# FFN up projection: four products of 512 columns and four of 256 per row tile, in four banks

## Chip, core and metric

The kernel runs on one core of a Trainium2 chip. The metric is the device time of one execution in microseconds (us). A core has TensorE (PE, matrix products into PSUM), VectorE (DVE), ScalarE (ACT), GpSimd (POOL) and SyncE (SP, which issues the loads here). PSUM has eight banks of 512 FP32 columns.

## What is computed

One block of a diffusion transformer on 256 latent and 256 context tokens of width 2048, in FP32. The first half (a modulated norm, an input projection, three mixers and an output projection) matters here only as what lies before. The second half is a convolutional FFN on the latent tokens:

```
def _conv_ffn(h, w_up, conv_w, conv_b, w_down, rows, width):
    gate, val = jnp.split(h @ w_up, 2, axis=-1)
    gate = lax.conv_general_dilated(gate.reshape(bsz, rows, width, D_FF), conv_w[:, :, None, :],
                                    (1, 1), 'SAME', feature_group_count=D_FF) + conv_b
    return (jax.nn.gelu(gate.reshape(bsz, l, D_FF)) * val) @ w_down

h_lat = h_lat + m_lat[5] * _conv_ffn(_modulate(h_lat, norm2_g[i], m_lat[3], m_lat[4]),
                                     ffn_w_up[i], ffn_conv_w[i], ffn_conv_b[i], ffn_w_down[i], rows, GRID_W)
return _rmsnorm(h_lat, norm_f)
```

(Calls are shortened.) `D_FF` is 5632, the grid has 4 rows of 64 tokens. `m_lat` are six vectors of 2048 made from the condition by a product with `ada_w`; `m_lat[5]` is the gate of the FFN.

## The kernel before

Activations lie with features on the 128 partitions and the 256 tokens along the free axis. FP32 products are made from a high and a low part of each operand: `split_w` (line 452) loads a block of weights (256 x 512, 512 KB), casts it to the type fp32r (ACT, line 457: the high part) and subtracts that from the block (DVE, line 459: the low part). `prod` (line 462) then makes three products into one place of PSUM: high weights by high activations (line 464), high by low (465), low by high (466). Every product loads its stationary operand (128 x 128 weights) anew and streams the activations.

`gemm_feat` (line 484) makes one group: 512 output columns over some blocks of weights, for each block two row tiles (128 input features each) by four blocks of 128 output columns. Its four sums, 256 tokens wide, share two PSUM banks (`two_banks`, line 472), taken in turn from a pool of four (`mm`). Another pool of three (`sm`) and one of a single bank (`ad`) serve the other tasks.

The FFN (`up` at line 1392, `down` at line 1422) has 11 units of 512 hidden features. `up(u)` makes a gate group and a value group of eight blocks each. The convolution reads the gate sums from PSUM: one scaled copy with bias (ACT, line 1403) and eight multiply-adds (DVE, line 1411) for each of four output blocks, in a buffer of the small pool `t`; then GELU, the product with the value sums (line 1418) and a split into high and low parts (lines 469 and 470). `down(g)` makes four groups over the hidden features of two units (of the last one alone) and adds them into `dsum` (lines 1437, 1439). The order is up 0, up 1, up 2, down 0, up 3, up 4, down 1, and so on. Activations for the up projection lie in eight tiles `f_t` (line 1352), four of high and four of low parts.

Vectors of `m_lat` are made beside that. `ada_vector` (line 419) is a task in turns: each turn loads 512 KB and multiplies and adds it on DVE (line 433), two halves of 16 turns; after each half two products with ones add up over partitions, into the bank `ad`. Two of the vectors are made so in the earlier stage, driven from its loops, and the last, the FFN gate, in the down groups (`t_gate`, line 1381). There its first half has to give back its buffer before the second can begin. Loads pass through rings of pages; the FFN uses four pages each for raw, high and low weights (line 1371) and three for `ada_w`.

A scheduler orders each engine's instructions before the run. It takes the order of the program as a priority, with the splitting of weights ahead by an offset (line 453); each engine runs its own list in order. So an edit in one task can change the neighbours on any engine.

Of the kernel before, what the change touches and what calls it, by code (L numbers as in the profile page):

```python
# [11 lines left out]
F32R = mybir.dt.float32r  # L12
AF = mybir.ActivationFunctionType
# [205 lines left out]
def tile_dit(ctx: ExitStack, tc: tile.TileContext, I, out: bass.AP, dbg=None):  # L219
# [198 lines left out]

    def ada_vector(c, after=None):

        ps = ada_bank()
        for half in range(2):
            tag = pages.take(4)
            acc = slot(tag, [P, 2, 512])
            if after is not None:

                V.tensor_copy(acc[:, 0, 0:1], after)
# [15 lines left out]
        ada_store(c, ps)  # L443
        yield

# [25 lines left out]

    def two_banks():
        bk = [mm_bank(), mm_bank()]
        return bk, lambda m: bk[m // 2][:, 256 * (m % 2):256 * (m % 2) + 256]
# [8 lines left out]

    def gemm_feat(w, cg, mv, between, kcs=None):
        kcs = list(range(8)) if kcs is None else kcs
        bk, at = two_banks()
# [864 lines left out]

    f_t = [[slot(pages.take(4), [P, 4, L], F32R) for _ in range(4)] for _ in range(2)]

    def f_of(kt):
        return f_t[0][kt // 4][:, kt % 4, :], f_t[1][kt // 4][:, kt % 4, :]

# [23 lines left out]

    t_gate = _Task(ada_vector(3, dsum[0][:, 0, 0:1]))

# [4 lines left out]
    def gated(cg):  # L1387
        for mt in range(4 * cg, 4 * cg + 4):
            V.scalar_tensor_tensor(h_of(mt), dsum[cg // 2][:, mt % 8, :], ada_cols[:, 3, mt:mt + 1], h_of(mt),
                                   ALU.mult, ALU.add)  # L1390

    def up(u, between):
        hd = hidden(u)
        bk, at = gemm_feat(I["w_up"], u, f_of, between)
        act = []
        for pr in range(2):
            acc = tb([P, 2, L])
            for e in range(2):
                m = 2 * pr + e
                mt = 4 * u + m  # L1400
                src = at(m).rearrange("p (r c) -> p r c", r=4)
                dst = acc[:, e, :].rearrange("p (r c) -> p r c", r=4)
                S.activation(acc[:, e, :], at(m), AF.Identity, bias=cw[:, 9, mt:mt + 1], scale=cw[:, 4, mt:mt + 1])  # L1403
                for dy in (-1, 0, 1):
# [98 lines left out]
```

## Time and profile before

| what | value |
|---|---|
| median of 3 runs | 1484.7 us (1481.24 to 1485.41) |
| the profiled execution | 1485.74 us, its span 1484.0 us |
| PE busy, products | 1429.8 us (96%), 11060 |
| DVE busy | 1070.7 us (72%) |
| ACT busy | 664.5 us (45%) |
| data moved | 318.57 MB, mean 215 GB/s |

Busy means that an engine had an instruction running. Products overlap in the pipeline of PE, so their durations add up to more than the time; the distance between the starts of neighbours is what one costs. The span is the profiled part of an execution, 1.7 us shorter than its time. FP32 products count twice in the profile. A granted clock of 1.00 is 2.4 GHz, 0.50 is 1.2 GHz.

### The profile page before, as it was taken

The page shows a single profiled execution, that of the slowest core. Times are in us where ns is not written, and L with a number is a line of the kernel's source. Part 1 is how long each engine was busy: PE and PEld are TensorE (multiplying, and loading weights), DVE is VectorE, ACT ScalarE, POOL GpSimd, SP SyncE. Part 2 cuts the span into 40 slices and gives each one's busy share as a digit, 9 for nine tenths or more (in the row PEclk, how much of TensorE's full clock was granted, in tenths as well). Part 3 has the DMA queues.
Part 4 walks back from the last instruction along what each step waited for, and adds up shares of the span by engine and source line. Part 5 has one row for each costly group of instructions (what it writes and reads, how often), then busy time and mean ns, then how long its engine had stood idle before and what let it go on. Part 6 is the DMA issues. An engine that isn't in the chain of part 4 may idle for free.

```text
span 1484.0 us, 27112 instructions
## 1 busy us (share of the span) xinstructions
PE 1429.8 (96%) x11060; PEld 1314.1 (89%) x11060; DVE 1070.7 (72%) x1774; ACT 664.5 (45%) x984; POOL 10.9 (1%) x9
## 2 busy tenths in 40 slices
PE   6998999999899999998999999999999999999997
PEld 3566696668888989998999999999999999999997
DVE  6568618997877888764867777675768787657766
ACT  6336851222568434343554444443444344434434
POOL 0000000000000000000000000000000000000000
PEclk9999999999999999998999999999999999999998
DMA  9788635667777787555465598666557866566552
GB/s 355 256 309 282 220 134 186 195 191 268 251 261 241 263 279 271 172 169 159 141 184 181 177 316 282 183 185 185 182 184 230 302 203 192 182 180 185 181 171 98
DMA packets 89956, 318.57 MB, mean 215 GB/s; under 512 B 12039, under 2 KB 12584, under 8 KB 89384
## 3 DMA queue, kind: packets, MB, share of 16 engines
q1 hardware_dynamic: 89832, 316.85, 65.1%
q8 instruction: 86, 1.41, 0.4%
q14 instruction: 38, 0.31, 0.1%
HBM read 312.62 MB, written 4.19 MB: 213 GB/s over the span
## 4 chain that ended last, share of the span: by engine, by line
PE 82%; DMA 7%; DVE 5%; ACT 3%; issue 2%; SPq 0%; DVEq 0%; ACTq 0%
PE mm L464 24%; PE mm L465 24%; PE mm L466 24%; DMA s4k<-in_ada_dram 6%; PE ad L410 2%; PE ad L373 2%; DVE s4k L433 1%; PE sm L579 1%; DVE s4k L459 1%; PE sm L855 1%; PE mm L339 1%; PE sm L311 1%; PE sm L549 1%; ACT s4k L457 1%; DMA s4k<-in_x_t_dram 1%
## 5 line engine op out<-in xcount | busy, mean ns | idle before, releaser
L457 ACT CAST s4k<-s4k 128x1024 fp32r<-128x1024 f32 x376 | 393.8, 1048 | 601.6 <-PE mm L465 420.7
L459 DVE TENSOR_TENSOR s4k<-s4k,s4k 128x1024 fp32r<-128x1024 f32 x376 | 459.0, 1222 | 252.8 <-ACT s4k L457 247.9
L464 PE MATMUL mm<-s4k,s4k 128*128 128x256 f32 (+1 forms) x2144 | 627.3, 295 | 4.8 <-ACT s4k L457 3.5
L466 PE MATMUL mm<-s4k,s4k 128*128 128x256 f32 (+1 forms) x2144 | 626.1, 294 | 4.9 <-DVE s4k L459 4.9
L465 PE MATMUL mm<-s4k,s4k 128*128 128x256 f32 (+1 forms) x2144 | 628.8, 294 | 1.5 <-DVE s4k L778 1.2
L464 PEld LDWEIGHTS mm<-s4k,s4k 128*128 128x128 f32 x2144 | 412.2, 193 | 28.9 <-issue 14.8
L466 PEld LDWEIGHTS mm<-s4k,s4k 128*128 128x128 f32 x2144 | 412.9, 193 | 19.9 <-DVE s4k L459 7.4
L465 PEld LDWEIGHTS mm<-s4k,s4k 128*128 128x128 f32 x2144 | 414.7, 193 | 16.4 <-issue 6.4
L464 PE MATMUL mm<-s8k,s4k 128*128 128x256 f32 x960 | 271.0, 283 | 0.8 <-ACT s8k L469 0.8
L465 PE MATMUL mm<-s8k,s4k 128*128 128x256 f32 x960 | 271.4, 283 | 0.0
L466 PE MATMUL mm<-s8k,s4k 128*128 128x256 f32 x960 | 269.9, 283 | 0.0
L464 PEld LDWEIGHTS mm<-s8k,s4k 128*128 128x128 f32 x960 | 183.9, 192 | 3.6 <-issue 2.5
L465 PEld LDWEIGHTS mm<-s8k,s4k 128*128 128x128 f32 x960 | 184.2, 192 | 0.3 <-DVE s8k L470 0.2
L466 PEld LDWEIGHTS mm<-s8k,s4k 128*128 128x128 f32 x960 | 183.5, 192 | 0.1
L433 DVE SCALAR_TENSOR_TENSOR s4k<-s4k,cs,s4k 128x1024 f32<-128x1024 f32 x90 | 115.4, 1282 | 49.2 <-DMA s4k<-in_ada_dram 48.8
L1411 DVE SCALAR_TENSOR_TENSOR t<-mm,s4k,t 128x189 f32<-128x189 f32 (+2 forms) x352 | 131.9, 423 | 7.9 <-ACT t L1403 6.3
L373 PE MATMUL ad<-s4k,cs 128*32 128x256 f32 x512 | 35.8, 393 | 6.6 <-DMA s4k<-in_ada_dram 5.8
L469 ACT CAST s8k<-t 128x512 fp32r<-128x512 f32 x38 | 23.2, 617 | 27.0 <-DVE t L1418 9.3
L373 PEld LDWEIGHTS ad<-s4k,cs 128*32 128x32 f32 x512 | 13.8, 110 | 21.2 <-DMA s4k<-in_ada_dram 7.3
L1403 ACT ACTIVATE t<-mm,s4k 128x256 f32<-128x256 f32 x44 | 24.7, 562 | 14.6 <-PE mm L466 13.6
L410 PE MATMUL ad<-s4k,cs 128*32 128x512 f32 x128 | 28.9, 604 | 1.0 <-DMA s4k<-in_ada_dram 0.5
L470 DVE TENSOR_TENSOR s8k<-t,s8k 128x512 fp32r<-128x512 f32 x38 | 25.8, 686 | 1.0
(285 smaller groups left out, 1045.2 us busy)
## 6 DMA issues: line engine op xcount, KB each, us to landing
s4k<-in_ada_dram SPq DMA_DIRECT2D x192, 512.0 KB, 4.9
s4k<-in_w_up_dram SPq DMA_DIRECT2D x176, 512.0 KB, 4.3
s4k<-in_w_down_dram SPq DMA_DIRECT2D x88, 512.0 KB, 3.7
s4k<-in_w_in_dram SPq DMA_DIRECT2D x80, 512.0 KB, 5.0
s4k<-in_w_out_dram SPq DMA_DIRECT2D x32, 512.0 KB, 3.9
s4k<-in_x_t_dram SPq DMA_DIRECT2D x8, 512.0 KB, 6.8
s4k<-in_ctx_t_dram SPq DMA_DIRECT2D x4, 512.0 KB, 10.2
hyk<-s8k SPq DMA_DIRECT2D x4, 512.0 KB, 4.1
```

The lines of the kernel that those rows point to most:

```text
L373: T.matmul(ps[32 * q:32 * q + 32, :], cs[:, 2 * k2 + e, :], raw[:, e, 256 * part:256 * part + 256], start=(k2 == 0), stop=(k2 == 7), skip_ ...
L410: T.matmul(ps[32 * q:32 * q + 32, :], cs[:, kt, :], raw[q // 2][:, q % 2, :], start=(kt == 0), stop=(kt == KT - 1), skip_group_check=True)
L433: V.scalar_tensor_tensor(acc, raw, cs[:, kt, 0:1], acc, ALU.mult, ALU.add)
L457: S.copy(h, raw)
L459: V.tensor_tensor(lo, raw, h.bitcast(F32), ALU.subtract)
L464: T.matmul(ps, a[0], b[0], start=first, stop=False, skip_group_check=True)
L465: T.matmul(ps, a[0], b[1], start=False, stop=False, skip_group_check=True)
L466: T.matmul(ps, a[1], b[0], start=False, stop=last, skip_group_check=True)
L469: S.copy(h, src)
L470: V.tensor_tensor(lo, src, h.bitcast(F32), ALU.subtract)
L1403: S.activation(acc[:, e, :], at(m), AF.Identity, bias=cw[:, 9, mt:mt + 1], scale=cw[:, 4, mt:mt + 1])
L1411: V.scalar_tensor_tensor(dst[:, r0:r1, c0:c1], src[:, r0 + dy:r1 + dy, c0 + dx:c1 + dx], cw[:, tap, mt:mt + 1], dst[:, r0:r1, c0:c1], ALU. ...
```

## The change

In the up projection the high and low activations of a row tile now lie side by side (`f_t` in eight tiles of two row tiles each), so that one product of 512 columns takes the high weights by both. `gemm_wide` makes, for each row tile, four such products (one per block of 128 output columns, each into a bank of its own, line 1429 of the new file) and then four of 256 columns with the low weights (line 1432). A group takes four banks: groups alternate between the four of `mm` and the three of `sm` with `ad` (`four_banks`). At its end ACT copies the high-by-low half out of each bank (line 1438) and DVE adds the other half (line 1439). The convolution and the product with the value now read those sums from SBUF; its result lies in a buffer `16k0`. `down` keeps `prod` and takes two banks a group from the set that the last up group left alone.

`ada_vector` loses three empty turns. The FFN gate has its own task `ada_gate2`, with one buffer for both halves and all its products with ones at the end, so that it no longer holds the bank `ad`.

```diff
-    def ada_vector(c, after=None):
+    def ada_vector(c):
...
-            yield
-            yield
             for e in range(2):
...
+            if half == 0:
+                yield
         ada_store(c, ps)
         yield
+
+    def ada_gate2(after):
+
+        acc = slot(pages.take(8), [P, 2, 2, 512])
+        V.tensor_copy(acc[:, 0, 0, 0:1], after)
+        for half in range(2):
+            for kt in range(KT):
+                raw = load_a(I["ada25"][3, kt, half])
...
+                    V.scalar_tensor_tensor(acc[:, half], raw, cs[:, kt, 0:1], acc[:, half], ALU.mult, ALU.add)
+                yield
+        yield
+        yield
+        ps = ada_bank()
+        for q in range(4):
+            T.matmul(ps[32 * q:32 * q + 32, :], ones[:, 0:1].to_broadcast([P, 32]), acc[:, q // 2, q % 2, :],
+                     start=True, stop=True, skip_group_check=True)
+        ada_store(3, ps)
...
-    f_t = [[slot(pages.take(4), [P, 4, L], F32R) for _ in range(4)] for _ in range(2)]
+    f_t = [slot(pages.take(4), [P, 2, 2, L], F32R) for _ in range(8)]
...
+    def f_both(kt):
+        return f_t[kt // 2][:, kt % 2, :, :].rearrange("p c n -> p (c n)")
...
-    t_gate = _Task(ada_vector(3, dsum[0][:, 0, 0:1]))
+    t_gate = _Task(ada_gate2(dsum[0][:, 0, 0:1]))
...
+    def four_banks():
+
+        bank_set[0] += 1
+        return [mm_bank() for _ in range(4)] if bank_set[0] % 2 else [sm_bank(), sm_bank(), sm_bank(), ada_bank()]
+
+    def gemm_wide(w, cg, between):
+
+        bk = four_banks()
+        for kc in range(8):
+            h, lo = split_w(w[cg, kc])
+            for kk in range(2):
+                kt = 2 * kc + kk
+                for m in range(4):
+                    ms = slice(128 * m, 128 * m + 128)
+                    T.matmul(bk[m], h[:, kk, ms], f_both(kt), start=(kt == 0), stop=False, skip_group_check=True)
+                for m in range(4):
+                    ms = slice(128 * m, 128 * m + 128)
+                    T.matmul(bk[m][:, :L], lo[:, kk, ms], f_of(kt)[0], start=False, stop=(kt == KT - 1),
+                             skip_group_check=True)
+            between()
+        both = [tb([P, 2, L]) for _ in range(2)]
+        for m in range(4):
+            t = both[m // 2][:, m % 2, :]
+            S.copy(t, bk[m][:, L:])
+            V.tensor_tensor(t, t, bk[m][:, :L], ALU.add)
+        return both
...
-        bk, at = gemm_feat(I["w_up"], u, f_of, between)
-        act = []
+        both = gemm_wide(I["w_up"], u, between)
+        act = slot("16k0", [P, 4, L])
...
-                src = at(m).rearrange("p (r c) -> p r c", r=4)
+                src = both[pr][:, e, :].rearrange("p (r c) -> p r c", r=4)
...
+        if g < len(groups) - 1:
+            bank_set[0] += 1
         for cg in range(4):
-            bk, at = gemm_feat(I["w_down"], cg, mv, lambda: with_down(g, cg), kcs)
+            if bank_set[0] % 2:
+                bk = [mm_bank(), mm_bank()]
+            else:
+                bk = [sm_bank(), sm_bank() if cg % 2 == 0 else ada_bank()]
+            bk, at = gemm_feat(I["w_down"], cg, mv, lambda: with_down(g, cg), kcs, bk)
```

The new file's lines are shifted: cast and subtraction of weights are 475 and 477 there, `prod` 482 to 484, the convolution's multiply-add 1462.

PE before, at the head of unit 3's gate group (out<-streamed, stationary; `s4k25` holds high activations, `s4k27` low ones, `s4k10` high weights, `s4k12` low ones; the last figure is the size of the result):

```order
L464 MATMUL mm_1192_9017<-s4k25_934_6829,s4k10_1195_9021 128x256
L465 MATMUL mm_1192_9017<-s4k27_938_6833,s4k10_1195_9021 128x256
L466 MATMUL mm_1192_9017<-s4k25_934_6829,s4k12_1196_9023 128x256
L464 MATMUL mm_1193_9018<-s4k25_934_6829,s4k10_1195_9021 128x256
L465 MATMUL mm_1193_9018<-s4k27_938_6833,s4k10_1195_9021 128x256
L466 MATMUL mm_1193_9018<-s4k25_934_6829,s4k12_1196_9023 128x256
```

The first two output blocks of the first bank, then of the second, each by three products. The same place in the change:

```order
L1429 MATMUL sm_1212_8701<-s4k25_934_6829,s4k10_1217_8707 128x512
L1429 MATMUL sm_1213_8702<-s4k25_934_6829,s4k10_1217_8707 128x512
L1429 MATMUL sm_1214_8703<-s4k25_934_6829,s4k10_1217_8707 128x512
L1429 MATMUL ad_1215_8704<-s4k25_934_6829,s4k10_1217_8707 128x512
L1432 MATMUL sm_1212_8701<-s4k25_934_6829,s4k12_1218_8709 128x256
L1432 MATMUL sm_1213_8702<-s4k25_934_6829,s4k12_1218_8709 128x256
L1432 MATMUL sm_1214_8703<-s4k25_934_6829,s4k12_1218_8709 128x256
L1432 MATMUL ad_1215_8704<-s4k25_934_6829,s4k12_1218_8709 128x256
```

Three rows per output block have become two, the first twice as wide, and neighbours write to four different banks.

DVE before, around the start of unit 3's convolution (`cs` marks the multiply-adds of the FFN gate vector, here the last two of its first half; `128x1024` without it is the subtraction of a block of weights):

```order
L459 TENSOR_TENSOR s4k_1217_9233<-s4k_1215_9229,s4k_1216_9231 128x1024
L433 SCALAR_TENSOR_TENSOR s4k_1150_8686<-s4k_1490_11785,cs,s4k_1150_8686 128x1024
L459 TENSOR_TENSOR s4k_1224_9305<-s4k_1222_9301,s4k_1223_9303 128x1024
L459 TENSOR_TENSOR s4k_1227_9335<-s4k_1225_9331,s4k_1226_9333 128x1024
L459 TENSOR_TENSOR s4k_1230_9365<-s4k_1228_9361,s4k_1229_9363 128x1024
L1411 SCALAR_TENSOR_TENSOR t_9259<-mm_9017,s4k_958_6901,t_9259 128x3x63
L1411 SCALAR_TENSOR_TENSOR t_9259<-mm_9017,s4k_958_6901,t_9259 128x192
L1411 SCALAR_TENSOR_TENSOR t_9259<-mm_9017,s4k_958_6901,t_9259 128x3x63
L459 TENSOR_TENSOR s4k_1233_9395<-s4k_1231_9391,s4k_1232_9393 128x1024
L1411 SCALAR_TENSOR_TENSOR t_9259<-mm_9017,s4k_958_6901,t_9259 128x4x63
L1411 SCALAR_TENSOR_TENSOR t_9279<-mm_9018,s4k_958_6901,t_9279 128x3x63
```

The same place in the change, from the last of the four sums on:

```order
L1439 TENSOR_TENSOR t_8882<-t_8882,ad_8704 128x256
L477 TENSOR_TENSOR s4k_1261_9026<-s4k_1259_9022,s4k_1260_9024 128x1024
L1462 SCALAR_TENSOR_TENSOR s16k_1242_8891<-t_8881,s4k_958_6901,s16k_1242_8891 128x3x63 x2
L1462 SCALAR_TENSOR_TENSOR s16k_1242_8891<-t_8882,s4k_958_6901,s16k_1242_8891 128x3x63
L453 SCALAR_TENSOR_TENSOR s8k_1170_8370<-s4k_1570_11309,cs,s8k_1170_8370 128x1024
L1462 SCALAR_TENSOR_TENSOR s16k_1242_8891<-t_8882,s4k_958_6901,s16k_1242_8891 128x3x63
L1462 SCALAR_TENSOR_TENSOR s16k_1242_8891<-t_8881,s4k_958_6901,s16k_1242_8891 128x192 x2
L477 TENSOR_TENSOR s4k_1264_9048<-s4k_1262_9044,s4k_1263_9046 128x1024
L1462 SCALAR_TENSOR_TENSOR s16k_1242_8891<-t_8882,s4k_958_6901,s16k_1242_8891 128x192 x2
L453 SCALAR_TENSOR_TENSOR s8k_1170_8370<-s4k_1579_11376,cs,s8k_1170_8370 128x1024
L1462 SCALAR_TENSOR_TENSOR s16k_1242_8891<-t_8881,s4k_958_6901,s16k_1242_8891 128x3x63
L477 TENSOR_TENSOR s4k_1267_9070<-s4k_1265_9066,s4k_1266_9068 128x1024
```

The sums of banks come first, the convolution reads the `t` tiles, and multiply-adds of the gate vector's second half (into `s8k`, line 453) stand among its steps, two to four steps apart.

ACT before, in the earlier stage, between 455 and 470 us of the profile (an `ACT_TABLE_LOAD` comes where the kind of function changes):

```order
L1110 ACT_TABLE_LOAD
L1110 ACTIVATE s16k_530_3717<-s16k_530_3717 128x2048 x2
L1133 ACT_TABLE_LOAD
L1133 ACTIVATE s8k_481_3371<-mm_3983 128x512
L1145 ACT_TABLE_LOAD
L1145 ACTIVATE s8k_626_4507<-s4k_629_4510,lg 128x256 x2
L457 CAST s4k_619_4443<-s4k_618_4441 128x1024
L457 CAST s4k_623_4476<-s4k_622_4474 128x1024
L1008 ACT_TABLE_LOAD
```

And in the change, from the same place on:

```order
L475 CAST s4k_618_4421<-s4k_617_4419 128x1024
L1123 ACTIVATE s16k_533_3730<-s4k_534_3731,lg 128x128 x6
L1026 ACT_TABLE_LOAD
L1026 ACTIVATE t_3709<-sm_3700,pk 128x256 x2
L1123 ACTIVATE s16k_533_3730<-s4k_534_3731,lg 128x128
L1026 ACTIVATE t_3724<-sm_3715,pk 128x256 x2
L1128 ACT_TABLE_LOAD
L1128 ACTIVATE s16k_533_3730<-s16k_533_3730 128x2048
L475 CAST s4k_623_4455<-s4k_622_4453 128x1024
L1128 ACTIVATE s16k_533_3730<-s16k_533_3730 128x2048
```

Before, exponentials (1110, 1145), a SiLU (1133) and a sigmoid (1008) take turns, with four table loads. Now the sigmoid (1026) comes ahead of the exponentials (1128), and this piece has two loads; over the whole list there are 19 before and 17 now.

## Rows read from the trace of the kernel before

**Rows 1.** The chain of work that ended last, shares of the span by engine.

```profile
PE 82%; DMA 7%; DVE 5%; ACT 3%; issue 2%; SPq 0%; DVEq 0%; ACTq 0%
```

**Rows 2.** Stretches of the span: length, then busy time and instructions of each engine.

```profile
core 0: us, PE busy (x) PEld busy (x) DVE busy (x) ACT busy (x) POOL busy (x), PEclk, DMA share, GB/s
0.00:705.60 705.60, 660.89 (x4687) 547.49 (x4687) 512.62 (x977) 322.10 (x591) 10.90 (x9) 0.98 0.69 235
705.60:1470.20 764.60, 764.60 (x6341) 762.66 (x6342) 551.05 (x783) 340.91 (x391) 0.00 (x0) 1.00 0.62 197
```

**Rows 3.** Waits in 706 to 1470 us: total us, times, longest us.

```profile
ACT s4k L457 <- PE mm L465: 345.8, 212, 2.4
...
DVE s4k L459 <- ACT s4k L457: 177.5, 172, 2.8
...
DVE s4k L433 <- DMA s4k<-in_ada_dram: 17.7, 19, 3.4
```

**Rows 4.** Groups by line and form, 700 to 1480 us: count, busy us, mean ns, idle before.

```profile
L464 PE MATMUL mm<-s4k,s4k 128*128 128x256 f32 x1408 | 399.2, 284 | 1.1 <-ACT s4k L1361 1.1
...
L464 PE MATMUL mm<-s8k,s4k 128*128 128x256 f32 x704 | 199.2, 283 | 0.0
```

**Rows 5.** Order of time on PE in the FFN: start us, us, instruction.

```profile
899.81 0.28 PE L465 MATMUL mm<-s4k,s4k 128*128 128x256 f32 x1
...
911.93 0.28 PE L464 MATMUL mm<-s4k,s4k 128*128 128x256 f32 x1
```

**Rows 6.** Order of time on PE in the stage of wide products.

```profile
298.82 0.39 PE L464 MATMUL mm<-s4k,s4k 128*128 128x512 f32 x1
...
302.68 0.39 PE L466 MATMUL mm<-s4k,s4k 128*128 128x512 f32 x1
```

**Rows 7.** The same stage, between products of other tasks.

```profile
309.40 0.40 PE L464 MATMUL mm<-s4k,s4k 128*128 128x512 f32 x1
...
311.49 0.39 PE L464 MATMUL mm<-s4k,s4k 128*128 128x512 f32 x1
```

**Rows 8.** The stretch at the start of the FFN.

```profile
706.00:712.00 6.00, 6.00 (x33) 6.00 (x33) 6.00 (x16) 3.81 (x8) 0.00 (x0) 0.58 0.00 0
```

**Rows 9.** Order of time on PE in that stretch.

```profile
705.96 0.41 PE L466 MATMUL mm<-s4k,s4k 128*128 128x256 f32 x1
...
711.05 0.28 PE L464 MATMUL mm<-s4k,s4k 128*128 128x256 f32 x1
```

**Rows 10.** Groups on DVE and on ACT, 700 to 1480 us.

```profile
L459 DVE TENSOR_TENSOR s4k<-s4k,s4k 128x1024 fp32r<-128x1024 f32 x260 | 317.8, 1223 | 180.4 <-ACT s4k L457 177.5 <-PE ad L440 1.7
...
L433 DVE SCALAR_TENSOR_TENSOR s4k<-s4k,cs,s4k 128x1024 f32<-128x1024 f32 x30 | 38.5, 1282 | 17.8 <-DMA s4k<-in_ada_dram 17.7
...
L1439 DVE TENSOR_TENSOR s8k<-s8k,mm 128x512 f32<-128x512 f32 x32 | 21.8, 685 | 0.4
...
L457 ACT CAST s4k<-s4k 128x1024 fp32r<-128x1024 f32 x260 | 272.5, 1048 | 389.1 <-PE mm L465 345.8 <-issue 28.3 <-DVE s4k L459 6.7
...
L1437 ACT COPY s8k<-mm 128x512 f32<-128x512 f32 x8 | 4.7, 583 | 4.9 <-PE mm L466 4.9
```

**Rows 11.** Stretches: convolution of a gate group on DVE, then the next group.

```profile
730.90:753.90 23.00, 23.00 (x194) 23.00 (x194) 21.12 (x41) 11.70 (x13) 0.00 (x0) 1.00 0.61 183
753.90:776.90 23.00, 23.00 (x194) 23.00 (x193) 12.15 (x12) 10.53 (x12) 0.00 (x0) 1.00 0.61 184
```

**Rows 12.** Groups on ACT, 420 to 510 us.

```profile
L1145 ACT ACT_TABLE_LOAD x2 | 2.6, 1283 | 0.0
```

**Rows 13.** The stretch of the earlier stage in which PE lacks work.

```profile
420.00:510.00 90.00, 83.84 (x604) 77.93 (x603) 69.00 (x101) 60.21 (x94) 0.00 (x0) 0.96 0.73 241
```

**Rows 14.** A stretch in which the FFN gate vector's loads run.

```profile
890.00:905.00 15.00, 15.00 (x128) 15.00 (x127) 11.59 (x11) 6.68 (x8) 0.00 (x0) 1.00 0.97 350
```

**Rows 15.** The stage of wide products: granted clock in the column after POOL.

```profile
298.82:313.00 14.18, 14.18 (x62) 9.14 (x60) 13.26 (x33) 3.29 (x5) 0.00 (x0) 1.00 0.52 152
```

More of the change, by code (lines that the diff above doesn't have):

```diff
@@ L424, in ada_vector @@
             acc = slot(tag, [P, 2, 512])
-            if after is not None:
-                V.tensor_copy(acc[:, 0, 0:1], after)
             for kt in range(KT):
@@ L442, in ada_vector @@
             pages.give(tag)
+            if half == 0:
+                yield
         ada_store(c, ps)
+        yield
[5 more added lines that the diff above has]
+                raw = load_a(I["ada25"][3, kt, half])
+                if kt == 0:
+                    V.tensor_scalar(acc[:, half], raw, cs[:, 0, 0:1], None, ALU.mult)
+                else:
+                    V.scalar_tensor_tensor(acc[:, half], raw, cs[:, kt, 0:1], acc[:, half], ALU.mult, ALU.add)
+                yield
+        yield
+        yield
+        ps = ada_bank()
[3 more added lines that the diff above has]
+        ada_store(3, ps)
         yield
@@ L470, in split_to, with two_banks @@
         V.tensor_tensor(lo, src, h.bitcast(F32), ALU.subtract)
-    def two_banks():
-        bk = [mm_bank(), mm_bank()]
+    def two_banks(bk=None):
+        bk = bk or [mm_bank(), mm_bank()]
         return bk, lambda m: bk[m // 2][:, 256 * (m % 2):256 * (m % 2) + 256]
@@ L482, in feat_block, with gemm_feat @@
                      mv(k0 + kk), first and kk == 0 and m % 2 == 0, last and kk == 1)
-    def gemm_feat(w, cg, mv, between, kcs=None):
+    def gemm_feat(w, cg, mv, between, kcs=None, banks=None):
         kcs = list(range(8)) if kcs is None else kcs
-        bk, at = two_banks()
+        bk, at = two_banks(banks)
         for n, kc in enumerate(kcs):
@@ L1350, in tile_dit @@
     r = inv_rms(sums, D, L)
-    f_t = [[slot(pages.take(4), [P, 4, L], F32R) for _ in range(4)] for _ in range(2)]
+    f_t = [slot(pages.take(4), [P, 2, 2, L], F32R) for _ in range(8)]
     def f_of(kt):
-        return f_t[0][kt // 4][:, kt % 4, :], f_t[1][kt // 4][:, kt % 4, :]
+        return f_t[kt // 2][:, kt % 2, 0, :], f_t[kt // 2][:, kt % 2, 1, :]
+    def f_both(kt):
+        return f_t[kt // 2][:, kt % 2, :, :].rearrange("p c n -> p (c n)")
     for kt in range(KT):
@@ L1390, in gated @@
                                    ALU.mult, ALU.add)
+    bank_set = [0]
+    def four_banks():
[21 more added lines that the diff above has]
+        return both
     def up(u, between):
         hd = hidden(u)
-        bk, at = gemm_feat(I["w_up"], u, f_of, between)
-        act = []
+        both = gemm_wide(I["w_up"], u, between)
+        act = slot("16k0", [P, 4, L])
         for pr in range(2):
-            acc = tb([P, 2, L])
+            acc = act[:, 2 * pr:2 * pr + 2, :]
             for e in range(2):
@@ L1400, in up @@
                 mt = 4 * u + m
-                src = at(m).rearrange("p (r c) -> p r c", r=4)
+                src = both[pr][:, e, :].rearrange("p (r c) -> p r c", r=4)
                 dst = acc[:, e, :].rearrange("p (r c) -> p r c", r=4)
-                S.activation(acc[:, e, :], at(m), AF.Identity, bias=cw[:, 9, mt:mt + 1], scale=cw[:, 4, mt:mt + 1])
+                S.activation(acc[:, e, :], both[pr][:, e, :], AF.Identity, bias=cw[:, 9, mt:mt + 1],
+                             scale=cw[:, 4, mt:mt + 1])
                 for dy in (-1, 0, 1):
@@ L1413, in up @@
             S.activation(acc, acc, AF.Gelu_apprx_tanh)
-            act.append(acc)
-        bk2, at2 = gemm_feat(I["w_up"], NU + u, f_of, between)
+        both = gemm_wide(I["w_up"], NU + u, between)
         for pr in range(2):
-            acc = act[pr].rearrange("p m n -> p (m n)")
-            V.tensor_tensor(acc, acc, bk2[pr], ALU.mult)
+            acc = act[:, 2 * pr:2 * pr + 2, :].rearrange("p m n -> p (m n)")
+            V.tensor_tensor(acc, acc, both[pr].rearrange("p m n -> p (m n)"), ALU.mult)
             ms = slice(2 * pr, 2 * pr + 2)
```

1 line of the change is left out of this document (added).

## The prediction

> **What bounds the kernel now.** I read the chain of waits first: TensorE (PE) makes up 82% of it [rows 1]. That is a mean over unlike stages, so next I cut the span into stretches [rows 2]. Up to 705.6 us PE is busy for 660.9 us and the other engines and the loads have their part in the end. From 705.6 to 1470.2 us, which is the FFN, PE is busy for all of 764.6 us at a granted clock of 1.00, while VectorE (DVE) is busy for 551.1 us and ScalarE (ACT) for 340.9 us. The waits of that stretch show who follows whom: the casts of the weights (ACT) stood for 345.8 us until PE gave a page back, and the subtractions (DVE) for 177.5 us behind the casts [rows 3]; no wait of PE itself is among them. So in the FFN only PE's own work counts. Of it, 3 x 1408 products belong to the up projection and 3 x 704 to the down projection [rows 4].
>
> What one product costs is not its recorded duration (283 ns, pipelined) but the distance between starts. Between 899.81 and 911.93 us lie 101 such distances: 12.12 / 101 = 120.0 ns for 256 columns [rows 5]. 6336 products at 120.0 ns are 760.3 us of the 764.6. At 2.4 GHz (a granted clock of 1.00) 256 columns are 106.7 ns; so each product carries 13.3 ns that do not depend on data. The earlier stage has products of 512 columns of the same type: 17 distances between 298.82 and 302.68 us, 3.86 / 17 = 227.1 ns [rows 6], which is 213.3 plus 13.8. The extra is paid per product, not per column.
>
> **The change, part by part.**
>
> *Up products.* For each of 1408 pairs of row tile and 128 output columns, three products of 256 columns become one of 512 and one of 256. Before: 3 x 120.0 = 360.0 ns. After: 227.1 + 120.0 = 347.1 ns. Gain 12.9 ns x 1408 = **18.2 us**, all of it on the path, since PE has no idle time here. Bounds: the widest gain is the whole 13.3 ns, 18.7 us. The least comes from a less even run of wide products, nine distances from 309.40 to 311.49 us, 232.2 ns each [rows 7]; 360.0 - 352.2 = 7.8 ns, 11.0 us. I take 227.1, because that run, like the FFN, has no foreign products in it, while the other lies between FP32 products of other tasks.
>
> The Trainium skill ("TensorE: Matmul & The Clock Gate", section on the back-to-back issue gap) puts the distance of isolated warm products at N / 2.4 plus about 2.5 ns, which would make the dropped product worth 1408 x 2.5 = 3.5 us, an estimate by that page. The 120.0 and 227.1 ns here stand 11 ns above that rule, and the measurement decides.
>
> *Start of the FFN.* The clock is low there: 0.58 on average over 706 to 712 us [rows 8]; 24 products from 705.96 to 711.05 us are 212 ns apart [rows 9], which is 256 columns at 1.2 GHz with nothing on top. Dropping products saves nothing in these 5 us (8 pairs x 13 ns = 0.1 us lost from the gain). The first wide product also needs the low half of its activation, where before the first narrow one ran without it. I charge 0.5 us for both, bounds 0 and 1.
>
> *Emptying the banks.* Each of 22 up groups now gets four copies (ACT, 256 columns from PSUM) and four sums (DVE, 256 columns), 88 of each. No row has just these shapes. The copy: from the 512-column copy (583 ns) and the 1024-column cast (1048 ns) a column costs 0.91 ns, so 256 columns take about 0.35 us; the upper end is 0.58. The sum: 685 ns at 512 and 1223 ns at 1024 columns, so about 0.42 us; the upper end is 0.69 [rows 10]. I take 0.35 and 0.42, the same operations at half the width. ACT grows by 31 us (to 51) and DVE by 37 us (to 61), against 424 and 214 us idle in the FFN. Cost on the path: **0**. What covers it is the alternation of two sets of four banks: a set is wanted again a whole group later, 64 x 0.347 = 22.2 us, and emptying it takes about 4 x 0.42 + 0.35 = 2.0 us. The down groups take the set that the last up group did not use.
>
> *DVE where it is fullest.* While the convolution of a gate group runs, DVE is busy for 21.1 of 23.0 us, and in the next group for 12.2 of 23.0 [rows 11]. With four sums the first becomes 22.8 us of work in 22.2 us, the second 13.8. So DVE is late by under 1 us in every other group, and gets it back. What would be late is convolution steps; the order above puts the subtractions of the weights in between, and they are made ahead. With four pages a cast begins when PE is through with the block four earlier, so its block starts three blocks later, 3 x 2.77 = 8.3 us; less cast and subtraction (1.05 + 1.22) there are 6.0 us to spare. Cost 0.
>
> *The FFN gate vector.* Its 32 loads and multiply-adds stay 32, at 1.28 us; what goes is the wait of the second half for the first half's products. In the order, the second 16 now stand among unit 3's convolutions instead of some groups later. Unit 3 then asks of DVE 21.1 + 12.2 + 8 x 0.42 + 16 x 1.28 = 57.1 us within 44.4. Convolution steps slide into unit 4's groups, where nothing on PE needs them; unit 3's hidden columns are first read in the second down pass, after unit 4. The subtractions stay at PE's pace but for some gaps, where two to four steps and one multiply-add lie between them: about 3.3 us against 2.77, at most ten times, 3 to 5 us late of the 6.0. Cost 0, bounds 0 and 7 (57.1 - 44.4 - 6.0).
>
> *Vectors of the earlier stage.* Each now lacks three turns of its task, so their loads and multiply-adds, and what the scheduler puts around them, move between 400 and 640 us; the products stay the same. The order of ACT has two table loads fewer there, 1.28 us each [rows 12]. PE lacked 90.0 - 83.8 = 6.2 us in 420 to 510 us [rows 13], partly waiting for casts. I take half of the two loads, **-1.3 us**; bounds -6.2 and +6.2.
>
> Sum against the profiled execution (1485.7 us, 1.0 above the median of 1484.7): 1485.7 - 18.2 + 0.5 - 1.3 = 1466.7. Taken to the median: **1465.7 us**.
>
> **Rivals.**
>
> *A. The gate vector's loads hold up the weights.* In the first 16 of them the transfers are already full: DMA share 0.97 at 350 GB/s in 890 to 905 us [rows 14], and 17.7 us of DVE's waiting was for them [rows 3]. Now 32 come with hardly a pause, in one queue with unit 3's weights, and DVE is crowded in the same place. For it: a block's weights and one such load are 1.05 MB per 2.8 us, 370 GB/s. Against it: PE did not wait in the first stretch. Price: 2 to 8 us, so about 1471 us.
>
> *B. The fixed 13 ns are not saved.* If a wide product costs two narrow ones, 240 ns, nothing is gained: 1484 us. Against it stands the 227.1 ns run [rows 6].
>
> *C. The banks are not empty in time (slower).* If PE stood at each of the 22 changes of set until the last sum is done, 2.0 us each, that is 44 us: 1465.7 + 44 = 1510 us. It decides the sign from 18.2 / 22 = 0.83 us per change on. It needs an emptying that lasts longer than a group, 22.2 us against 2.0, or two groups in a row on one set, and the program's count of sets excludes the latter. The four-bank stage with wide products before shows a granted clock of 1.00 [rows 15], so rotating through four banks has not slowed PE there. The Trainium skill (same page, section on the second HAM failure mode) reports a 512-column kernel that cycles through banks and loses its clock by small idle gaps; the stage just named does not show that.
>
> *D. The shifted earlier stage costs its upper bound,* +6.2 instead of -1.3: 1473 us.
>
> **How the numbers follow.** Chances: the sum 0.70, A 0.15, D 0.07, B 0.05, C 0.03. Faster or slower counts from 0.3%, 4.5 us, on, about what a measurement of this kernel can tell from no change. The sum, A and D lie below 1480: 0.92 faster, 0.05 same, 0.03 slower. Range: downwards the full 13.3 ns (0.5 us) and 5 of the earlier stage's 6.2 us, 1460; upwards the least gain (11.0 instead of 18.2: 1473) and most of A, 1475. B and C lie outside, and so do corners of the others.
>
> **What would show it.** Up products 227 and 120 ns apart and a pair at 347; the FFN some 18 us shorter, about 747 us from its first to its last product; PE busy all through it; DVE at about 79% of it; the subtractions still waiting for casts, and these for PE. A is right if PE waits for casts or subtractions near unit 3 or 4; C if it waits at the heads of groups; D if the stretch before the FFN is longer than 706 us. The forecast falls if wide products in the FFN stand 232 ns or more apart.

## The result, and the profile after

The changed kernel takes 1467.49 us (median of 4 runs, 1463.34 to 1468.38), the kernel before in the same comparison 1484.08 us (1481.24 to 1485.41): ratio 0.9885, 95% interval 0.9861 to 0.9909. A second comparison on another chip gave 0.9890 (0.9867 to 0.9913). The forecast was 1465.7 in 1460 to 1475, so the sign, the size and the range held. The term that carries the forecast came out 5 us smaller than forecast, and lesser ones, not foreseen at their size, made up for most of it.

The profiled execution took 1467.65 us, 18.1 less than the one before (1485.74). The page's busy times and its chain by engine:

```profile
PE 1411.5 (96%) x9652; PEld 1236.4 (84%) x9652; DVE 1091.3 (74%) x1861; ACT 683.8 (47%) x1070; POOL 10.9 (1%) x9
...
PE 83%; DVE 7%; DMA 5%; ACT 3%; issue 1%; SPq 0%; DVEq 0%; ACTq 0%
```

TensorE (PE) holds the chain as it did in [rows 1], with 1408 products fewer (9652 for 11060). Now the FFN, from its first up product to the start of the last sum of squares (L311), in windows of the changed kernel; the columns are those of [rows 2]:

```profile
0.00:702.11 702.11, 657.20 (x4685) 545.75 (x4685) 512.90 (x977) 319.87 (x589) 10.90 (x9) 0.98 0.69 236
...
702.11:1452.78 750.67, 750.67 (x4940) 687.35 (x4941) 571.83 (x872) 362.41 (x479) 0.00 (x0) 1.00 0.60 201
```

and the same two stretches of the kernel before:

```profile
0.00:704.55 704.55, 660.08 (x4684) 546.97 (x4685) 511.57 (x974) 321.05 (x589) 10.90 (x9) 0.98 0.70 235
...
704.55:1470.89 766.34, 766.10 (x6348) 763.87 (x6349) 552.61 (x788) 341.96 (x393) 0.00 (x0) 1.00 0.62 197
```

The FFN became 15.7 us shorter, the stages ahead 2.4 us, and the tail behind it is 13.1 us in both. PE is busy in all 750.67 us. VectorE (DVE) went from 552.6 to 571.8 us, 76% of them where some 79% was foreseen, and ScalarE (ACT) from 342.0 to 362.4. PE's own waits, from just ahead of the FFN to the end:

```profile
PE sm L311 <- DVE s4k L1344: 2.2, 1, 2.2
PE mm L1429 <- DVE s4k L1383: 2.1, 1, 2.1
PE sm L321 <- DVE t L318: 1.2, 2, 0.6
```

The first and third belong to the norm. The second is the first wide product, which waits for the low half of its activation. No group head waits for a bank, no product for a weight. The rest is pitch, the distance from the start of one product to the start of the next. PE in order of time, at the place of [rows 5]:

```profile
900.02 0.86 PE L1429 MATMUL sm<-s4k,s4k 128*128 128x512 f32 x3
900.73 0.39 PE L1429 MATMUL ad<-s4k,s4k 128*128 128x512 f32 x1
900.95 0.52 PE L1432 MATMUL sm<-s4k,s4k 128*128 128x256 f32 x3
901.31 0.28 PE L1432 MATMUL ad<-s4k,s4k 128*128 128x256 f32 x1
901.43 0.86 PE L1429 MATMUL sm<-s4k,s4k 128*128 128x512 f32 x3
```

One row tile lasts from 900.02 to 901.43 us, 1.41 us. Over all row tiles at full clock, from the starts in the trace, a wide product takes 232.0 ns, a narrow one 118.6, a pair 350.6, where the forecast had 227.1 + 120.0 = 347.1. The gain per pair is 360.0 - 350.6 = 9.4 ns, times 1408 = **13.2 us** for the 18.2 forecast.

The work that empties the banks, groups of ACT and then of DVE in the FFN (busy us, mean ns):

```profile
L1438 ACT COPY t<-mm 128x256 f32<-128x256 f32 x44 | 13.1, 382 | 0.0
...
L1438 ACT COPY t<-sm 128x256 f32<-128x256 f32 x33 | 10.1, 377 | 0.0
```

```profile
L1439 DVE TENSOR_TENSOR t<-t,mm 128x256 f32<-128x256 f32 x44 | 15.8, 416 | 0.0
...
L1439 DVE TENSOR_TENSOR t<-t,sm 128x256 f32<-128x256 f32 x33 | 11.9, 415 | 0.0
```

0.38 and 0.42 us stand where 0.35 and 0.42 had been estimated.

### The profile page after: what moved, and what is told of

It is laid out like the page before. It is cut to its first block, busy times and chain, and to the rows that moved or that the text cites. A ratio compares the mean times of both kernels' runs of the same rounds, so it can differ in the third digit from the quotient of the medians.

```text
span 1465.9 us, 24451 instructions
## 1 busy us (share of the span) xinstructions
PE 1411.5 (96%) x9652; PEld 1236.4 (84%) x9652; DVE 1091.3 (74%) x1861; ACT 683.8 (47%) x1070; POOL 10.9 (1%) x9
## 3 DMA queue, kind: packets, MB, share of 16 engines
HBM read 312.62 MB, written 4.19 MB: 216 GB/s over the span
## 4 chain that ended last, share of the span: by engine, by line
PE 83%; DVE 7%; DMA 5%; ACT 3%; issue 1%; SPq 0%; DVEq 0%; ACTq 0%
PE mm L1429 11%; PE mm L482 11%; PE mm L484 10%; PE mm L483 10%; PE sm L1429 8%; PE mm L1432 6%; PE sm L1432 4%; DMA s4k<-in_ada_dram 4%; PE ad L1429 3%; PE sm L482 2%; PE sm L483 2%; PE sm L484 2%; PE ad L410 2%; PE ad L1432 1%; DVE s4k L430 1%
## 5 line engine op out<-in xcount | busy, mean ns | idle before, releaser
L477 DVE TENSOR_TENSOR s4k<-s4k,s4k 128x1024 fp32r<-128x1024 f32 x376 | 459.0, 1222 | 229.0 <-ACT s4k L475 228.5
L482 PE MATMUL mm<-s4k,s4k 128*128 128x256 f32 (+1 forms) x736 | 226.7, 315 | 4.0 <-ACT s4k L475 3.8
L483 PE MATMUL mm<-s4k,s4k 128*128 128x256 f32 (+1 forms) x736 | 227.6, 312 | 1.2 <-DVE s4k L796 1.2
L484 PE MATMUL mm<-s4k,s4k 128*128 128x256 f32 (+1 forms) x736 | 226.0, 312 | 2.8 <-DVE s4k L477 2.8
L482 PE MATMUL mm<-s8k,s4k 128*128 128x256 f32 x704 | 199.8, 285 | 3.8 <-DVE s4k L1309 3.8
L483 PE MATMUL mm<-s8k,s4k 128*128 128x256 f32 x704 | 200.0, 285 | 0.0
L484 PE MATMUL mm<-s8k,s4k 128*128 128x256 f32 x704 | 199.5, 284 | 0.0
L1429 PE MATMUL mm<-s4k,s4k 128*128 128x512 f32 x704 | 193.5, 397 | 2.1 <-DVE s4k L1383 2.1
L482 PEld LDWEIGHTS mm<-s4k,s4k 128*128 128x128 f32 x736 | 139.6, 192 | 28.9 <-issue 15.8
L483 PEld LDWEIGHTS mm<-s4k,s4k 128*128 128x128 f32 x736 | 141.5, 192 | 15.9 <-issue 7.4
L484 PEld LDWEIGHTS mm<-s4k,s4k 128*128 128x128 f32 x736 | 140.3, 192 | 16.8 <-issue 5.7
L1429 PE MATMUL sm<-s4k,s4k 128*128 128x512 f32 x528 | 151.5, 395 | 0.0
L482 PEld LDWEIGHTS mm<-s8k,s4k 128*128 128x128 f32 x704 | 136.0, 194 | 4.9 <-issue 4.8
L1429 PEld LDWEIGHTS mm<-s4k,s4k 128*128 128x128 f32 x704 | 121.4, 190 | 18.6 <-DVE s4k L1383 2.4
L483 PEld LDWEIGHTS mm<-s8k,s4k 128*128 128x128 f32 x704 | 136.2, 194 | 0.0
L484 PEld LDWEIGHTS mm<-s8k,s4k 128*128 128x128 f32 x704 | 135.9, 193 | 0.1
L1462 DVE SCALAR_TENSOR_TENSOR s16k<-t,s4k,s16k 128x189 f32<-128x189 f32 (+2 forms) x352 | 129.7, 429 | 0.0
L1432 PEld LDWEIGHTS mm<-s4k,s4k 128*128 128x128 f32 x704 | 108.4, 189 | 15.2
L1432 PE MATMUL mm<-s4k,s4k 128*128 128x256 f32 x704 | 112.4, 282 | 0.0
L1432 PEld LDWEIGHTS sm<-s4k,s4k 128*128 128x128 f32 x528 | 87.0, 188 | 15.1
L430 DVE SCALAR_TENSOR_TENSOR s4k<-s4k,cs,s4k 128x1024 f32<-128x1024 f32 x60 | 76.9, 1282 | 25.3 <-DMA s4k<-in_ada_dram 25.2
```

The costliest lines, as they stand in the source:

```text
L477: V.tensor_tensor(lo, raw, h.bitcast(F32), ALU.subtract)
L482: T.matmul(ps, a[0], b[0], start=first, stop=False, skip_group_check=True)
L483: T.matmul(ps, a[0], b[1], start=False, stop=False, skip_group_check=True)
L484: T.matmul(ps, a[1], b[0], start=False, stop=last, skip_group_check=True)
L1429: T.matmul(bk[m], h[:, kk, ms], f_both(kt), start=(kt == 0), stop=False, skip_group_check=True)
L1432: T.matmul(bk[m][:, :L], lo[:, kk, ms], f_of(kt)[0], start=False, stop=(kt == KT - 1), skip_group_check=True)
```

## The experiments

FFN times below run, as above, from the first up product to the first L311 behind the last product. Each ratio is to the kernel before, on the same chip. The times in the expectations start from the changed kernel's 1467 us on the first chip, where the kernel before took 1484.1; on the chips of the runs below it takes 1480.4 to 1480.5. So what can be compared between runs is the ratio, the pitch and the length of the FFN.

**1. The vectors alone.** The kernel before with the changed `ada_vector` and with the gate vector as its own task:

```diff
-    t_gate = _Task(ada_vector(3, dsum[0][:, 0, 0:1]))
+    t_gate = _Task(ada_gate2(dsum[0][:, 0, 0:1]))
```

> The kernel before with the two edits of the modulation vectors alone (the changed ada_vector and the new ada_gate2); up and down as before. If the gain is the wide products' (my theory), the stages ahead of the FFN end about 2.4 us earlier, as they do in the changed kernel (702.1 for 704.6), the FFN keeps its 766 us and its 120.0 ns products, and the time is 1482 us (1479 to 1485), 0.2% under the kernel before. If the vectors carry the gain (rival), the FFN itself is shorter and the time is under 1476.

Measured: 1496.44 us (1495.49 to 1498.17), ratio 1.0112 (1.0099 to 1.0126). Both expectations missed. PE's waits and two windows of this kernel tell why:

```profile
PE mm L482 <- DVE t L1429: 13.3, 1, 13.3
```

```profile
920.00:935.00 15.00, 15.00 (x123) 14.19 (x122) 14.81 (x20) 6.37 (x7) 0.00 (x0) 1.00 0.96 344
935.00:950.00 15.00, 1.71 (x9) 1.50 (x8) 12.33 (x22) 1.45 (x3) 0.00 (x0) 0.63 0.75 249
```

The gate vector's multiply-adds now come in one clump, all between 855.8 and 955.1 us, where in the kernel before the second half waited for the first half's products on PE (at 1145.7 us) and its last came at 1185.4. DVE is busy for 14.81 of 15 us, its convolution steps (L1429, 352 of them) fall behind, and they read the bank itself. PE, two groups on, wants that bank and stands for 13.3 us; the granted clock then falls (0.63 over this window). The FFN took 781.2 us for 766.3. The changed kernel has the same clump and DVE is as full there, but PE works through:

```profile
920.00:935.00 15.00, 15.00 (x88) 13.10 (x87) 15.00 (x25) 6.53 (x10) 0.00 (x0) 1.00 0.87 290
935.00:950.00 15.00, 15.00 (x87) 13.07 (x86) 14.98 (x23) 5.80 (x7) 0.00 (x0) 1.00 0.87 301
```

Its convolution reads the copies in SBUF, and the bank is free after one copy and one sum. Run 2 has the same vectors and as many products at the same pitch, but the changed kernel's banks and copies, and PE does not wait there. So this part of the change loses 16 us by itself and nothing beside the rest.

**2. Three narrow products in four banks.** The changed kernel, its two sets, copies, sums and vectors, with the wide product split in two:

```diff
-                    T.matmul(bk[m], h[:, kk, ms], f_both(kt), start=(kt == 0), stop=False, skip_group_check=True)
+                    T.matmul(bk[m][:, :L], h[:, kk, ms], fh, start=(kt == 0), stop=False, skip_group_check=True)
+                    T.matmul(bk[m][:, L:], h[:, kk, ms], fl, start=False, stop=(kt == KT - 1), skip_group_check=True)
```

> The changed kernel with its four banks a group, its two sets, its copies and sums, but with two products of 256 columns in the place of each wide one. If the price is that of the product, not of the columns (my theory), three products of 120.0 ns stand where a pair of wide and narrow took about 350.6 ns: 1408 x 9.4 ns = 13 us are lost, and the time is 1480.5 (1478 to 1483). If the gain is that of the four banks and the later emptying (rival), the time stays at 1467 to 1470. If emptying costs something beside the products, it stands over the kernel with the vectors alone, here in these two runs.

Measured: 1481.8 us (1476.17 to 1484.86), ratio 1.0005 (0.9991 to 1.0019). The whole gain is gone: the banks, the emptying and the vectors together are worth nothing that this can tell. Products are 120 ns apart again, and the FFN lasts from 698.31 to 1462.05 us, 763.7; against 750.7 that is 13.1 us for 1408 products, 9.3 ns each, as the pitch says. The medians differ by more, some 18 us if the changed kernel's ratio is applied to this chip; what the executions other than the profiled ones did is not in a trace, and those 5 us stay open. (The profiled execution, 1476.89 us, is the second fastest of the eleven.)

**3. Width changing at every product.** Each block's wide product, then at once its narrow one:

```diff
                 for m in range(4):
                     ms = slice(128 * m, 128 * m + 128)
                     T.matmul(bk[m], h[:, kk, ms], f_both(kt), start=(kt == 0), stop=False, skip_group_check=True)
-                for m in range(4):
-                    ms = slice(128 * m, 128 * m + 128)
                     T.matmul(bk[m][:, :L], lo[:, kk, ms], f_of(kt)[0], start=False, stop=(kt == KT - 1),
```

> The changed kernel with each block's wide product followed at once by its narrow one, into the same bank: eight changes of width a row tile for two. Theory: what a wide product takes above the 227 ns of an unbroken run comes from the change of width; a row tile takes 1402.6 ns for 4 x 226.8 + 4 x 120.0 = 1387, so a change of width costs about 7.6 ns, six more changes cost 46 ns a row tile, 352 x 46 ns = 16 us, and the time is 1483 (1475 to 1485). Rival (a wide product in four changing banks costs 231 ns whatever stands beside it): the time stays at 1467 to 1469.

Measured: 1468.07 us (1467.7 to 1471.05), ratio 0.9924 (0.9911 to 0.9936). The theory's 1483 is missed. The time lies where the rival had it, but that was worked out from the first chip, and the rival's price is wrong too: wide products took 236.0 ns for its 231, narrow ones 117.0, a pair 353.0; the FFN 754.2 us, 3.5 more than in the changed kernel. A change of width does cost, but not a fixed sum each time.

**4. Runs of eight.** Both row tiles of a page wide, then both narrow:

```diff
                 for m in range(4):
                     ms = slice(128 * m, 128 * m + 128)
                     T.matmul(bk[m], h[:, kk, ms], f_both(kt), start=(kt == 0), stop=False, skip_group_check=True)
+            for kk in range(2):
+                kt = 2 * kc + kk
                 for m in range(4):
                     ms = slice(128 * m, 128 * m + 128)
                     T.matmul(bk[m][:, :L], lo[:, kk, ms], f_of(kt)[0], start=False, stop=(kt == KT - 1),
```

> The changed kernel with the order of a page changed: eight wide products (both row tiles of a page), then the eight narrow ones; half as many changes of width. If a change of width costs 7.6 ns (theory), a row tile saves 7.6 ns, 352 x 7.6 = 2.7 us, and the time is 1464.8 (1463.5 to 1466.5). If the cost goes with the bank that changes at every product (rival), the time stays at 1467 to 1468.

Measured: 1462.95 us (1461.31 to 1467.59), ratio 0.9890 (0.9872 to 0.9908): by the total not to be told from the changed kernel. By the pitch it is: wide 230.1, narrow 119.1, a pair 349.2 ns; the FFN 748.5 us, 2.2 less, where 2.7 was expected.

**5. Runs of sixteen.** On odd pages the narrow products come first:

```diff
+        for part in ((narrows, wides) if turn else (wides, narrows)):
+            part()
```

> The changed kernel with eight wide and then eight narrow products on even pages, eight narrow and then eight wide on odd ones: runs of sixteen of one width. A row tile took 26 ns above 4 x 227 + 4 x 120 with runs of one, 15 with runs of four, 9 with runs of eight; if what is lost is lost at the head of each run (theory), runs of sixteen lose about 5, a row tile takes 1392 to 1394 ns, and the time is 3 to 4 us under the changed kernel, 1463 to 1464.5, ratio 0.986. If what remains comes from the banks that change (rival), it is that of the runs of eight.

Measured: 1461.68 us (1460.35 to 1467.09), ratio 0.9883 (0.9852 to 0.9913); wide 228.5, narrow 119.5, a pair 348.0 ns, 1392 a row tile as expected; the FFN 746.5 us, 4.2 less than the changed kernel's. The ratio alone can't be told from that kernel's 0.9885. One run of sixteen, in the set whose bank names differ, so that every fourth product has a row of its own:

```profile
727.84 0.86 PE L1426 MATMUL sm<-s4k,s4k 128*128 128x512 f32 x3
728.54 0.40 PE L1426 MATMUL ad<-s4k,s4k 128*128 128x512 f32 x1
728.77 0.85 PE L1426 MATMUL sm<-s4k,s4k 128*128 128x512 f32 x3
729.46 0.39 PE L1426 MATMUL ad<-s4k,s4k 128*128 128x512 f32 x1
729.68 0.84 PE L1426 MATMUL sm<-s4k,s4k 128*128 128x512 f32 x3
730.36 0.39 PE L1426 MATMUL ad<-s4k,s4k 128*128 128x512 f32 x1
730.59 0.62 PE L1426 MATMUL sm<-s4k,s4k 128*128 128x512 f32 x2
```

The first three take 0.70 us, the same three later 0.68 (729.68 to 730.36). Product by product the starts give 233, 236, 228, 233, 230 ns at the head of the run and 226 or 227 from the sixth on. The bank changes at every product to the end of the run, and the second eight use a new block of weights; so it is neither that costs, but the place in the run. With 226.7 ns for a wide product deep in a run and 120.0 for a narrow one, a run of wide products and the narrow ones behind it lose 6 ns in runs of one, 16 in runs of four, 20 in runs of eight and 21 in runs of sixteen: the loss grows with the run until its first five products are through, and no further.

**6. One set of banks.** All up groups on the same four banks, the down groups on the other four (all but the last):

```diff
-        return [mm_bank() for _ in range(4)] if bank_set[0] % 2 else [sm_bank(), sm_bank(), sm_bank(), ada_bank()]
+        return [mm_bank() for _ in range(4)]
```

> The changed kernel with all up groups on the same four banks (the down groups keep the other four). 17 of the 22 up groups then follow another on the same banks and start only when the first bank's copy (0.38 us) and sum (0.42 us) are done, and go on at the pace of the sums (0.42 us a bank for 0.23 us a product). If the second set is what keeps emptying off the path (my theory), each of the 17 heads shows a wait of 1 to 3 us and the time is 1467 + 17 x 1.5 to 17 x 3 = 1493 to 1518 us. If the early copy alone is enough (rival), the heads show under 0.3 us each and the time stays under 1473.

Measured: 1529.86 us (1528.54 to 1536.79), ratio 1.0344 (1.0315 to 1.0374). PE's waits have the 17 heads, and the order of time shows one; behind it the granted clock is 0.57 on average to 757.00 us:

```profile
PE mm L1429 <- DVE t L1439: 40.8, 17, 4.5
```

```profile
753.61 0.50 PE L1429 MATMUL mm<-s4k,s4k 128*128 128x512 f32 x1 [2.30 <-DVE t L1439]
753.95 0.31 PE L1432 MATMUL mm<-s4k,s4k 128*128 128x256 f32 x1
754.07 0.62 PE L1429 MATMUL mm<-s4k,s4k 128*128 128x512 f32 x1
754.49 0.41 PE L1432 MATMUL mm<-s4k,s4k 128*128 128x256 f32 x1
754.70 0.63 PE L1429 MATMUL mm<-s4k,s4k 128*128 128x512 f32 x1
```

40.8 / 17 = 2.4 us a group head (the first product of a group), within the 1 to 3 us expected; with stretches of low clock behind many of them (mean 0.97 over the FFN) the FFN takes 813 us for 751, and the time lies above the 1493 to 1518 that the waits alone would give. This is rival C: 2.0 us a head had been estimated, without the clock. What keeps it away is the second set.

**7. Emptying twice over.** A further copy on each engine, in SBUF, for each of the 88 blocks:

```diff
             S.copy(t, bk[m][:, L:])
+            V.tensor_copy(t, t)
+            S.copy(t, t)
             V.tensor_tensor(t, t, bk[m][:, :L], ALU.add)
```

> The changed kernel with the copy of each block done once more on the vector engine and once more on the scalar engine, in SBUF, before the sum: 88 x some 0.4 us more for each engine, at the very place where banks are emptied. If emptying lies beside the products with room to spare (my theory), the time stays within 0.3% of the changed kernel's, 1463 to 1471 us. If it is just covered (rival), a group near the gate vector's loads, where the vector engine already was busy for 20.00 of 20 us, waits for its banks: a wait of some 5 to 13 us on TensorE there and 1475 to 1490 us.

Measured: 1466.42 us (1465.5 to 1473.17), ratio 0.9916 (0.9888 to 0.9945). ACT did 29.2 us more and DVE 21.8; the FFN took 751.0 us for 750.7. The clump is full to the brim, and PE does not wait:

```profile
920.00:970.00 50.00, 50.00 (x289) 43.82 (x288) 49.86 (x79) 27.53 (x42) 0.00 (x0) 1.00 0.88 300
```

So emptying lies beside the products, with room for these further copies.

**8. Down products wide too.** Hidden units are stored with high and low halves side by side; ten of eleven units' down products go wide and narrow, on alternating sets:

```diff
+                            T.matmul(bk[m], h[:, kk, ms], hid_both(kt), start=(n == 0 and kk == 0), stop=False,
...
+                            T.matmul(bk[m][:, :L], lo[:, kk, ms], mv(kt)[0], start=False,
```

> The changed kernel with the down products of all groups but the last wide and narrow too, on four banks a group in alternating sets: 640 of the remaining 704 block steps, 640 x 9.4 ns = 6 us less on TensorE. If the price is that of the product (theory), the time is 1461.5 us (1459.5 to 1464), ratio 0.984 to 0.985. The vector engine gets eight sums of 0.42 us for two of 0.69 a column group, some 39 us more over 20 of them; if it is the bound near the gate vector's loads (rival), TensorE waits there, as it did for 13.9 us with the vectors alone, and the time is 1470 to 1485.

Measured: 1456.5 us (1455.26 to 1459.81), ratio 0.9843 (0.9821 to 0.9864). The FFN lasts 745.3 us (694.56 to 1439.84), 5.4 less where 6.0 was worked out. The time lies 3.0 us under the expected range, but the ratio is in its own: the range of the time had been worked out from the first chip. DVE is busy for 49.99 of 50 us (920 to 970 us) in the clump, and PE waits for nothing there. (The wait with the vectors alone is 13.3 us in the trace of run 1, not 13.9.)

**9. Both.** Wide down products and runs of sixteen:

> Both that were faster at once: wide products in up and in all down groups but the last, and runs of sixteen of one width. If the two gains are both TensorE's and add (theory), 2048 block steps stand 348.1 ns apart for 351.2 with the wide down groups alone: 2048 x 3.1 = 6.3 us less than that kernel's 1456.5, 1450 us (1448 to 1453), ratio 0.979 to 0.982. If the vector engine or the loads bound the down groups by now (rival), a wait for a bank or for a weight page appears on TensorE and the time stays at 1454 or above. A narrow run ahead on odd pages needs the low half first, so a late subtract would show as a wait of a narrow product.

Measured: 1452.43 us (1447.91 to 1454.68), ratio 0.9810 (0.9786 to 0.9833); the FFN 740.2 us (696.28 to 1436.48), pairs 348.1 ns apart, no wait of PE in it but the first. The two gains add, 10.5 us of FFN together; 5.1 of them are the gain over run 8, where 6.3 was worked out. This is faster than both kernels of the case: 1463.76 us for the changed one beside it.

**10. The changed kernel once more**, beside run 9:

> The changed kernel itself, on the chip of the run beside it. Its ratio to the kernel before should be 0.9885 again (0.986 to 0.991), some 1464 to 1468 us; a row tile of 1400 to 1406 ns in the up groups again. If these pitches were a matter of the one execution (rival), they would come out otherwise here.

Measured: 1463.76 us (1461.8 to 1465.43), ratio 0.9890 (0.9867 to 0.9913); pairs 350.8 ns apart; the FFN 750.4 us. The pitch of a pair repeats to 0.2 ns and the FFN to 0.3 us. The stage ahead doesn't: it ended at 697.18 us here and at 702.11 in the first profile, with the same program.

## Why the prediction was right, and where it was not

- *What bounds the FFN.* Right. PE is busy all through; only the price of products counted. Run 2 shows it alone: all other parts of the change kept and the wide product split, and the gain is gone.
- *Up products, 18.2 us.* The mechanism was right, the size was not: 13.2 us, 9.4 ns a pair. The step that failed is the choice of 227.1 ns [rows 6] over 232.2 [rows 7], "because that run, like the FFN, has no foreign products in it". What decided was the place in the run. [rows 6] lies deep in a long run of wide products, [rows 7] at the head of one, and the FFN's come in runs of four, all of them head. The run of [rows 6] begins at 295.53 us; that of [rows 7] has eleven products between foreign ones (L1083):

```profile
295.53 0.50 PE L465 MATMUL mm<-s4k,s4k 128*128 128x512 f32 x1
...
308.95 0.38 PE L1083 MATMUL sm<-s8k,s8k 128*128 128x128 f32 x2
309.09 0.48 PE L466 MATMUL mm<-s4k,s4k 128*128 128x512 f32 x1
...
311.72 0.38 PE L1083 MATMUL sm<-s8k,s8k 128*128 128x128 f32 x2
```

  Foreign products end a run, and how long the head behind them lasts varies: in the run from 295.53 us the distances are 226 or 227 ns from the fourth product on, in one from 305.85 us only from the eleventh, and in that of [rows 7] they stay between 224 and 236 to its end. So that 232.2 came so near the FFN's mean is in part chance. This mean, 232.0 ns, is the figure at which the text said the forecast falls; this term did fall by 5 us, and the narrow products at 118.6 for 120.0 ns gave a little back. The Trainium skill ("TensorE: Matmul & The Clock Gate", section on the back-to-back issue gap) would have the dropped product at an estimated 2.5 ns; run 2 measured 9.3.
- *Start of the FFN, +0.5.* The wait for the low half is there: from the norm's last products (L321) to the first up product 3.37 us for 2.33. It lies ahead of the FFN as cut above. Inside, the low clock ended earlier. Windows of the kernel before, then of the changed one:

```profile
704.55:711.00 6.45, 6.21 (x27) 5.92 (x28) 6.45 (x18) 3.96 (x9) 0.00 (x0) 0.50 0.00 0
```

```profile
702.11:706.30 4.19, 4.19 (x12) 3.52 (x13) 4.19 (x11) 1.93 (x5) 0.00 (x0) 0.50 0.00 0
```

  6.45 us at a granted clock of 0.50 became 4.19. At 212 for 120 ns a product [rows 9] that is 1.0 us of the FFN; the second product's wait of 0.24 us is gone too. In the repeat the low clock lasted some 3 us. This was not forecast; together the three make 1.04 - 1.0 - 0.24 = -0.2 us for the +0.5. Why the clock rose earlier is not shown.
- *The gate vector, 0.* No stall, so right for this kernel. But the reason given, steps that "slide into unit 4's groups, where nothing on PE needs them", holds only because the bank is emptied ahead of the convolution; run 1 shows the 13.3 us that the same slide costs where it is not. What was missed is a small gain: the FP32 products with ones (two records each) now visit PE once, all eight records together, and not twice with four. One visit of the kernel before, then the one of the changed kernel:

```profile
1145.45 0.28 PE L466 MATMUL mm<-s8k,s4k 128*128 128x256 f32 x1
1145.66 1.05 PE L440 MATMUL ad<-s4k,ones 128*32 128x512 f32 x4
1146.64 0.38 PE L464 MATMUL mm<-s8k,s4k 128*128 128x256 f32 x1
1146.86 0.28 PE L465 MATMUL mm<-s8k,s4k 128*128 128x256 f32 x1
```

```profile
1410.73 0.28 PE L484 MATMUL mm<-s8k,s4k 128*128 128x256 f32 x1
1410.94 1.06 PE L459 MATMUL ad<-s8k,ones 128*32 128x512 f32 x8
1411.93 0.38 PE L482 MATMUL mm<-s8k,s4k 128*128 128x256 f32 x1
1412.16 0.28 PE L483 MATMUL mm<-s8k,s4k 128*128 128x256 f32 x1
```

  Two distances of 120 ns are 0.24 us; here they took 1.41 and 1.43. A visit costs 1.2 us whether four or eight records come, and one of two is gone.
- *Emptying, and DVE where it is fullest, 0.* Right: run 7 empties more at no cost, and run 6 shows what it costs without the second set.
- *Earlier stage, -1.3.* 2.4 us shorter in the first profile, 7.4 in the second (697.18 for 704.55). The program is the same in both, so this term can't be told from what that stage varies by. In all eleven profiles of kernels with the changed vectors it ended between 694.56 and 703.29 us; the kernel before has one profile, 704.55.
- *The sum.* 13.2 (products) + 1.2 (one visit) + 1.3 (low clock and second product at the start: 1.0 + 0.2 by rows, 0.1 unassigned) + 2.4 (ahead) = 18.1 us, which is the difference of the two profiled executions; forecast were 18.2 - 0.5 + 1.3 = 19.0. 5 us too much in the one term were nearly made up by three small ones, none of which was foreseen at its size. That the total came so close is luck: the earlier stage varies by more than those 2.4 us, and with the second profile of the changed kernel, 1462.95 us, the difference would have been 22.8.
- *Rivals.* A (loads): PE waits for no weight or cast; false here. B: a wide product took 232.0 ns, not 240; false. C: false because of the second set; without it, true at 2.4 us a group, 3.7 with the low clock that follows. D: the stage ahead did not grow; false.

## What to carry to other kernels

The price per product is paid on every product, so fewer and wider ones gain even where PE never waits; read the wide pitch from the head of a run or from deep in it, as the products will stand in the new kernel. A change whose parts lean on each other can't be judged part by part: the later, denser gate vector loses 16 us alone and nothing where banks are emptied into SBUF at once. When the vector engine is full for a stretch, ask who holds a bank while it catches up. Here two sets of banks, emptied early, took that stretch off TensorE's path.

## What was not expected of the hardware

After a stretch of narrow products the first five wide ones took 233, 236, 228, 232 and 231 ns between starts and the sixth and later 226.7, as means over the runs of sixteen of run 5, with hardly any scatter; the runs of eight of run 4 begin in the same way. In runs of four and of one the mean was 232.0 and 236.0. The first narrow product of a run was a little shorter, 113 to 118 ns. Why is not shown; the banks changed throughout, so it is not that (run 5).

A wait at a group's head cost more than its length: 40.8 us of waits in run 6, 62 us more of FFN. Behind the head at 753.61 us, shown above, a wide product took 0.42 us for 0.23 (754.07 to 754.49) and a narrow one 0.21 for 0.12.

Eight records of FP32 products with 32 output rows (four products of the program) took no longer on PE's path than four: 1.43 us against 1.41 with the distances around them.
